# Neighbourhood-attention layer: a cap on the bytes that the attention stage's DMAs have under way

## The chip, the cores and the metric

The kernel runs on one core of a Trainium2 chip. The metric is device time in microseconds (us) of one execution; three timed runs of the kernel before gave 990.62, 991.14 and 992.26 us, median 991.14. A further execution was profiled, and all profile lines come from it.

## The reference

The reference is one pre-norm residual layer (DEPTH is 1, so only mixer A is used) on x of 2048 tokens by 1024 channels in float32, with 16 heads of 64 channels and the tokens laid out as a grid of 32 rows by 64 columns:

```
h = rmsnorm(x, norm_0)
q, k, v, gate = split(h @ w_in_0, 4)             # w_in_0: 1024 x 4096
o = neighbourhood_attention(q, k, v, rpb_0)      # each token: 8 x 16 neighbours of the grid, learned bias
x = x + (o * silu(gate)) @ w_out_0               # w_out_0: 1024 x 1024
return rmsnorm(x, norm_f)
```

Inside the attention each query sees 8 rows by 16 columns of keys; scores get a per-head relative-position bias, a softmax, and weight the values.

## The kernel before

All matmuls work on float32 data that is split into a high and a low float32r part, three products for one. The projections and the output projection use a seven-product (Strassen) scheme on quarters. The order of the instructions is fixed while the program is built: `build` runs through the work once, and a queue of delayed actions (`store(key, lag, f)`, run by `due` as the count of issued matmuls goes on) decides where stores and loads stand between the other instructions.

The program has three stages in time. Up to about 561 us, `stage_one` and `stage_two` make the projections; q, k, the gate and v are stored to DRAM tensors (`qd`, `kd`, `sgd`, `vd`). From 561 to 871 us runs the attention, in `cycles` = 32 cycles of about 9.7 us; from 871 us on, the last part of the output projection (`rows_by_seven`) with the final norm.

In the attention, a cycle m works on one pair of heads p and one quarter T of the tokens, taken from the list `order`. PE does four things in it: some matmuls of the rest of the projections (`group`, tile `pp`, L384 to L388) or, later, of the output projection (tile `po`, L1600 to L1604), as filling; transposes of the normalised probabilities of the cycle before (`turns`, tile `ph`, L1372); the scores of this cycle (`scores`, tile `s`, L1323); and the weighted values of the cycle before (`values`, tile `o`, L1395). These four stand in this order, so the transposes, scores and values form one uninterrupted burst of short matmuls at the end of every cycle. ACT, DVE and POOL do the exponentials, the normalisation and the copies out of PSUM.

The data of a cycle come by DMA from SP's queue. `begin(m)` puts them in the queue at the start of cycle m: the gate tile of the cycle before (`load_sg`, tile `sgt`, L1263), two bias tables (`load_bias`, `em`, L1277), the queries (`load_q`, tile `q`, L1248) and keys (`load_k`, `kt`, L1239) of the next cycle, and the values of this one (`load_v`, `vt`, L1258). Beside them stand the store of the finished tile (`keep`, `ogd<-og`, L1402), loads of weights (`load_item`, `raw`, L161 and L163), and stores of the last projections (`give`, L366 and L373). q, k and v have two buffers each, so a load of q waits until the scores that read its buffer are done, and a load of v until the weighted values that read its buffer are done. Most are of 256 KB; `vt` is 480 KB, `kt` 128 to 512 KB, `em` 184 or 253 KB. From cycle 24 on, finished rows of the attention are loaded back (`load_og`, tile `ograw`, L1429), split by ACT and DVE (`split_og`, L1441) and multiplied by the output weights. In the last cycle nine tiles of prepared weights (`land_first`, tile `t`, L1624) and six tiles of attention rows (`load_rows_of`, `raw<-ogd`, L1656) are loaded for the part after the attention, whose products stand in L1695 and read what `form_rows` (L1661 on ACT, L1662 on DVE) makes of those rows.

SP issues its DMAs strictly in the order of the program. Each DMA signals one of eight semaphores, DMAHW0 to DMAHW7, in turn, and before it is issued it waits for the last DMA on the same semaphore, the one eight places earlier. So at most eight are under way.

Of the kernel before, what the change touches and what calls it, by code (L numbers as in the profile page):

```python
# [31 lines left out]
RES_BUFS, RES_EARLY = 3, 1  # L32
PLAIN = 4

FRAME, TALL = [0, 4, 12, 17], 15
# [26 lines left out]
def build(ctx, tc, x, xr, xt, wg, bias, w_out, n0, nf, out):  # L62
    nc = tc.nc
# [90 lines left out]
    def load_item(it):  # L154
        kind, a, b = it
        t = raws[it] = raw([128, 512], F32, "raw")
        asked_at[it] = now()
        if kind == "x":
            nc.sync.dma_start(t, xt[a * 128:(a + 1) * 128, b * 512:(b + 1) * 512])
        elif kind == "w":  # L160
            nc.sync.dma_start(t, wg[a[0], :, 512 * b:512 * b + 512])  # L161
        else:
            nc.sync.dma_start(t, w_out[a * 128:(a + 1) * 128, b * 512:(b + 1) * 512])  # L163

# [191 lines left out]
    def give(kind, hp, c, t, bank_=False):  # L356
        while sum(e[1][0] in "kqg" for e in later) > 1:
            later.pop(0)[2]()
        s = slice(c * 512, c * 512 + 512)
        written.add((kind, hp, c))  # L360
        to, at = (lambda o: lay(kind, o), of(kind, t)) if bank_ else (lambda o: o, t)
        if kind == "g":
            sg = ev([128, 512], F32, "sg")
            nc.scalar.activation(to(sg), at, AF.Tanh, scale=0.5)
            nc.vector.scalar_tensor_tensor(to(sg), to(sg), 1.0, at, op0=OP.add, op1=OP.mult)
            store(("g", hp, c), 12, lambda: nc.sync.dma_start(sgd[hp][c], sg))  # L366
# [6 lines left out]
        store((kind, hp, c), 12, lambda: nc.sync.dma_start(qd[hp][c] if kind == "q" else kd[hp][:, s], t))  # L373

# [22 lines left out]
    def put_rows(dst, v):  # L397
        nc.sync.dma_start(dst, v.rearrange("p (h d) -> p h d", h=4))

# [13 lines left out]
    def seven_products(us, c0, X1, also):  # L413
# [5 lines left out]
        def load_w(n, f, home=raw):  # L419
            A[n, f] = home([128, 512], F32, "raw")  # L420
            k, j = us[n]
            b = 512 * quarter[f]
            nc.sync.dma_start(A[n, f], wg[KINDS[k] + j, :, b:b + 512])

# [110 lines left out]
    def load_x(c0, f, k, to, cols=slice(0, 512)):  # L535
        r, c = int(f[1]) - 1, int(f[2]) - 1 + c0
        nc.sync.dma_start(to[:, cols], xt[(4 * r + k) * 128:(4 * r + k + 1) * 128, c * 512 + cols.start:c * 512 + cols.stop])

# [48 lines left out]
    def load_s(q, *js):  # L587
        for j in js:
            if q in vsp:
                a, b = j % 2, j // 2  # L590
                if a == 0:
                    W[q, b] = wp([128, 2, 512], F32R, "wh"), wp([128, 2, 512], F32R, "wl")
                for i, t in enumerate(W[q, b]):
                    nc.sync.dma_start(t[:, :, a * 256:a * 256 + 256].bitcast(F32), vsp[q][j, i].rearrange("p (k c) -> p k c", c=256))
                continue
            VR[q, j] = t = raw([128, 512], F32, "raw")
            nc.sync.dma_start(t, wg[KINDS["v"] + 2 + j % 2, :, 1024 + 512 * (j // 2):1536 + 512 * (j // 2)] if q == "A22" else vsd[q][j])

# [18 lines left out]
    def stage_one():  # L617
# [24 lines left out]
        def load_rows(c, hs, p):  # L642
            for h in hs:
                t, j = 4 * c + h // 2, h % 2
                rows_in[t, j] = p([128, 512], F32, "row")
                nc.sync.dma_start(rows_in[t, j], xr[t * 128:t * 128 + 128, 512 * j:512 * j + 512])

# [7 lines left out]
        def value_rows(j):  # L655
            spot = mkp([128, 3, 512], F32, "vs")
            homes = [spot[:, k] for k in range(3)] + [kh([128, 512], F32, "vs")]
            a, b = j % 2, j // 2
            for f, u, h in (("A21", 1, 0), ("A22", 1, 2), ("A11", 0, 0), ("A12", 0, 2)):
                VS[f] = homes.pop()  # L660
                o = 512 * (b + h)
                nc.sync.dma_start(VS[f], wg[KINDS["v"] + 2 * u + a, :, o:o + 512])

        def value_sum(j, f):
            a, b, to, o = {"S1": ("A21", "A22", "A22", OP.add), "S3": ("A11", "A21", "A21", OP.subtract),
                           "S2": ("S1", "A11", "A11", OP.subtract), "S4": ("A12", "S2", "A12", OP.subtract)}[f]
            nc.vector.tensor_tensor(VS[to], VS[a], VS[b], o)
            VS[f] = s = VS[to]
            if f in vsd:
                store(("vs", f, j), 3, lambda: nc.sync.dma_start(vsd[f][j], s))  # L670

        def value_split(j, f):
            h, l = ev([128, 512], F32R, "vsh"), ev([128, 512], F32R, "vsl")
            split_to(h, l, VS[f], None)
            for i, s in enumerate((h, l)):
                store(("vs", f, j, i), 5, lambda i=i, s=s: nc.sync.dma_start(vsp[f][j, i], s.bitcast(F32)))

        def ask_rows(m):
            more_rows[m] = xp([128, 512], F32, "row"), xp([128, 512], F32, "row")
            for j in range(2):  # L680
                nc.sync.dma_start(more_rows[m][j], xr[(8 + m) * 128:(9 + m) * 128, 512 * j:512 * j + 512])

# [113 lines left out]
        for t in range(4):  # L796
            u = ev([128, 512], F32, "u1v")
            nc.scalar.activation(u, ps[t], AF.Copy)
            nc.sync.dma_start(vu1[t], u)
        load_rows(0, range(8), mp)  # L800
# [119 lines left out]
        def load_u1():  # L920
            for t in range(4):
                U1[t] = accs[t] if t < 2 else ep([128, 528], F32, "u1")[:, :512] if t == 2 else kh([128, 512], F32, "u1")
                nc.sync.dma_start(U1[t], vu1[t])

# [86 lines left out]
    def stage_two():  # L1011
# [11 lines left out]
        def out_rows(k):  # L1023
            def g():
# [7 lines left out]
                for q, (r_, c_) in quarters.items():  # L1032
                    OW[q] = homes.pop()
                    nc.sync.dma_start(OW[q], w_out[(4 * r_ + k) * 128:(4 * r_ + k + 1) * 128, c_ * 512:c_ * 512 + 512])
            return g
# [8 lines left out]
        def out_split(k, f):  # L1044
            def g():
# [3 lines left out]
                for i, s in enumerate((h, l)):  # L1049
                    store(("ow", f, k, i), 5, lambda i=i, s=s: nc.sync.dma_start(wod[f][k, i], s.bitcast(F32)))  # L1050
            return g
# [174 lines left out]
    def load_k(p, T):  # L1226
# [5 lines left out]
        def keys():  # L1232
# [4 lines left out]
            if T == 2:  # L1237
                nc.gpsimd.memset(t[:, 1280:1288], 0.0)
            nc.sync.dma_start(t[:, a - base * GW:b - base * GW], kd[p][:, a:b])  # L1239

        return keys

    def load_q(p, T):
        must(("q", p, T))

        def queries():
            QT[p, T] = qp([128, 512], F32, "q")
            nc.sync.dma_start(QT[p, T], qd[p][T])  # L1248

        return queries  # L1250

    def load_v(p, T):
# [4 lines left out]
        VT[p, T] = t.rearrange("p (s d) -> p s d", s=8)  # L1257
        nc.sync.dma_start(t[:8 * TALL], rows)  # L1258

    def load_sg(p, T):  # L1260
        must(("g", p, T))
        SG[p, T] = sp([128, 512], F32, "sgt")
        nc.sync.dma_start(SG[p, T], sgd[p][T])  # L1263

# [3 lines left out]
    def load_bias(p, T):  # L1268
# [4 lines left out]
        for quad in range(2):  # L1273
            t = mp([128, 512], F32, "em")[:, :w]
            EM[p, T // 2, kind].append([t[:, :w // 2], t[:, w // 2:]])
            o = TABLE_AT[kind] + quad * w
            fs.append(lambda t=t, o=o, w=w: nc.sync.dma_start(t, bias[p, 128 * o:128 * (o + w)].rearrange("(q c) -> q c", c=w)))  # L1277
        return fs
# [103 lines left out]
    def values(m):  # L1382
# [18 lines left out]
        def keep():  # L1401
            nc.sync.dma_start(ogd[T][:, p // 4, :, p % 4].rearrange("i a q -> a i q"), og.rearrange("p (i q) -> p i q", i=4))  # L1402
            written.add(("og", p, T))
# [7 lines left out]
    def late_loads():  # L1411
        for j in range(2):
            nc.sync.dma_start(accs[j], bass.AP(tensor=nf.tensor, offset=nf.offset + 512 * j,
                                               ap=[[0, 128], [1, 512]]))
# [10 lines left out]
    def load_og(n):  # L1425
        T, i = divmod(n, 4)
        must(*[("og", p, T) for p in range(NP)])
        G[n] = t = wp([128, NK, 128], F32, "ograw")
        nc.sync.dma_start(t.rearrange("p (h k) q -> p h k q", h=2), ogd[T][i].rearrange("h a k q -> a h k q"))  # L1429

    def load_res(n, j):
        RES[n, j] = rbp([128, 512], F32, "xr")
        nc.sync.dma_start(RES[n, j], x[n * 128:n * 128 + 128, 512 * j:512 * j + 512])

# [186 lines left out]
    def land(where, homes):  # L1621
        for (f, k, i), h in zip(where, homes):
            TF.setdefault(f, [[None, None] for _ in range(4)])[k][i] = h
            nc.sync.dma_start(h.bitcast(F32), wod[f][k, i])  # L1624

# [25 lines left out]
    def load_rows_of(m, f, home=None):  # L1651
# [3 lines left out]
        A[m, f] = (home or raw)([128, 512], F32, "raw")  # L1655
        nc.sync.dma_start(A[m, f].rearrange("p (k q) -> p k q", k=4), ogd[T][i, half])  # L1656

# [12 lines left out]
    def load_rest_of(m):  # L1670
        n = PAIRS[m][0]
        RES[n, 0] = rbp([128, 512], F32, "xr")
        nc.sync.dma_start(RES[n, 0], x[n * 128:n * 128 + 128, :512])

# [150 lines left out]
    for m in range(cycles + 1):  # L1825
        a = amount[m] - 8
        begin(m)
        feed(HALF_HEAD)
# [89 lines left out]
```

## Time and profile before

| | |
|---|---|
| three timed runs | 990.62, 991.14, 992.26 us; median 991.14 |
| the profiled execution | 993.25 us |
| its span, first to last instruction | 991.5 us |
| PE busy | 979.3 us, 99% of the span |
| DVE, ACT, POOL busy | 755.2, 531.5, 159.6 us |
| bytes moved by DMA | 227.93 MB, mean 230 GB/s |
| granted TensorE clock | 0.999 |

Of a row of a DMA listing, the last number is the median time in us from issue to landing. In a list of instructions the first number is the start in us from the start of the span, the second the time in us, and what stands in brackets is how long the engine sat idle before and what ended that. In the chain of work that ended last, "issue" is time in which an engine waited for nothing that the profile shows. A table by stretches gives for each stretch the busy time of each engine with its instructions, the granted clock, the busy share of the DMA engines and the GB/s they moved.

### The profile page before, as it was taken

To read this page: it belongs to the slowest core of one execution; us is meant where nothing else is said; L and a number is where in the kernel's file an instruction comes from. 1 tells how busy PE (TensorE), PEld (TensorE's weight loads), DVE (VectorE), ACT (ScalarE), POOL (GpSimd) and SP (SyncE) were. 2 spreads that over 40 slices of the span, in tenths; PEclk is the share of its full clock that TensorE was granted. 3 is DMA by queue.
4 is the path that set the end of the run, shared out by engine and by line. 5 is a ranking of instruction groups with operands and counts; after the bars stand their busy time and mean duration, and the time that the engine had idled before them with its cause. 6 is when DMAs were issued, how large, how long until landed. Compare 5 with 4: busy or idle time off the path is not lost.

```text
span 991.5 us, 22624 instructions
## 1 busy us (share of the span) xinstructions
PE 979.3 (99%) x8172; PEld 797.0 (80%) x8172; DVE 755.2 (76%) x1735; ACT 531.5 (54%) x1310; POOL 159.6 (16%) x430
## 2 busy tenths in 40 slices
PE   9999999999999999999999999999999999999997
PEld 7888888888888888888888778777778777888886
DVE  6899888988665876766775677668778878877866
ACT  7773245455535342343433467677777776654443
POOL 0000001231100000000001133333343332302110
PEclk9999999999999999999999999999999999999999
DMA  8943547777957836657565799878989978697754
GB/s 287 337 130 102 196 132 256 248 242 251 368 159 225 276 116 201 189 182 224 169 176 203 247 302 271 264 226 279 307 277 288 298 222 266 223 379 212 205 146 117
DMA packets 149968, 227.93 MB, mean 230 GB/s; under 512 B 13536, under 2 KB 66016, under 8 KB 149856
## 3 DMA queue, kind: packets, MB, share of 16 engines
q1 hardware_dynamic: 146832, 221.37, 70.2%
q0 software_dynamic: 2592, 4.72, 2.8%
q8 instruction: 64, 1.05, 0.4%
q14 instruction: 48, 0.39, 0.1%
q10 hardware_dynamic: 432, 0.40, 0.1%
HBM read 160.37 MB, written 66.06 MB: 228 GB/s over the span
## 4 chain that ended last, share of the span: by engine, by line
PE 99%; issue 1%; DVE 0%; ACT 0%
PE pp L446 40%; PE pv L612 13%; PE py L1695 12%; PE o L1395 8%; PE s L1323 6%; PE ph L1372 5%; PE pp L388 2%; PE pp L384 2%; PE pp L386 2%; PE pv L727 2%; PE po L1600 2%; PE po L1604 2%; PE po L1602 2%; PE zp L127 0%; PE prb L235 0%
## 5 line engine op out<-in xcount | busy, mean ns | idle before, releaser
L446 PE MATMUL pp<-h,f 128*128 128x512 f32 x576 | 185.3, 389 | 0.0
L446 PE MATMUL pp<-t,f 128*128 128x512 f32 x702 | 171.4, 389 | 0.0
L446 PEld LDWEIGHTS pp<-t,f 128*128 128x128 f32 x702 | 131.8, 188 | 27.4
L1340 ACT ACTIVATE x<-sums,st 128x264 f32<-128x264 f32 (+1 forms) x256 | 124.5, 488 | 30.0 <-DVE st L1332 30.0
L446 PEld LDWEIGHTS pp<-h,f 128*128 128x128 f32 x576 | 108.1, 188 | 22.6
L446 PE MATMUL pp<-l,f 128*128 128x512 f32 x288 | 112.0, 389 | 0.0
L1352 POOL TENSOR_SCALAR x<-x,st 128x264 f32<-128x264 f32 (+1 forms) x192 | 88.5, 477 | 113.7 <-DVE st L1347 93.8
L1332 DVE CUSTOM_DVE_ANT_0 sums<-s,em 128x253 f32<-128x253 f32 (+1 forms) x256 | 91.1, 401 | 6.2 <-ACT x L1340 1.7
L429 DVE TENSOR_TENSOR f<-raw,f 128x512 fp32r<-128x512 f32 x105 | 75.9, 727 | 19.4 <-ACT f L428 19.3
L1395 PE MATMUL o<-pta,vt 120*64 120x192 f32 (+2 forms) x1152 | 85.1, 300 | 4.0 <-issue 4.0
L1395 PEld LDWEIGHTS o<-pta,vt 120*64 120x64 f32 x1152 | 70.2, 137 | 23.2 <-issue 16.4
L428 ACT ACTIVATE f<-raw 128x512 fp32r<-128x512 f32 x105 | 63.4, 622 | 36.6 <-DVE raw L435 22.0
L1376 DVE COPY pta<-ph 120x512 f32<-120x512 f32 x96 | 60.3, 684 | 18.3 <-PE ph L1372 18.1
L1378 ACT ACTIVATE pta<-ph 120x512 f32<-120x512 f32 x96 | 50.4, 599 | 37.8 <-PE ph L1372 37.8
L446 PEld LDWEIGHTS pp<-l,f 128*128 128x128 f32 x288 | 54.0, 188 | 11.3
L1323 PE MATMUL s<-kt,q 64*32 64x253 f32 (+1 forms) x2048 | 59.2, 362 | 0.7 <-issue 0.7
L1372 PEld LDWEIGHTS ph<-ident,x 64*120 64x120 f32 x1536 | 47.6, 135 | 11.3 <-issue 10.6
L612 PE MATMUL pv<-wh,t 128*128 128x512 f32 x176 | 56.2, 389 | 0.0
L1695 PE MATMUL py<-woh,f 128*128 128x512 f32 x168 | 55.4, 390 | 0.0
L467 POOL TENSOR_TENSOR tmp<-tmp,rb 128x512 f32<-128x512 f32 x18 | 28.5, 1582 | 157.6 <-DVE tmp L464 137.2
L446 PE MATMUL pp<-sixths,f 128*128 128x512 f32 x198 | 52.7, 389 | 0.0
L1372 PE MATMUL ph<-ident,x 64*120 64x64 f32 x1536 | 52.0, 221 | 0.0
(231 smaller groups left out, 1889.4 us busy)
## 6 DMA issues: line engine op xcount, KB each, us to landing
raw<-in_wg_dram SPq DMA_DIRECT2D x124, 256.0 KB, 4.8
vt<-vd SPq DMA_DIRECT2D x32, 480.0 KB, 5.2
row<-in_xr_dram SPq DMA_DIRECT2D x32, 256.0 KB, 5.2
vd<-v SPq DMA_DIRECT2D x32, 256.0 KB, 3.2
sgd<-sg SPq DMA_DIRECT2D x32, 256.0 KB, 3.8
q<-qd SPq DMA_DIRECT2D x32, 256.0 KB, 3.6
sgt<-sgd SPq DMA_DIRECT2D x32, 256.0 KB, 5.3
ogd<-og SPq DMA_DIRECT2D x32, 256.0 KB, 5.3
```

The costliest lines, as they stand in the source:

```text
L428: nc.scalar.activation(t[:, 0], src, AF.Copy)
L429: nc.vector.tensor_tensor(t[:, 1], src, t[:, 0].bitcast(F32), OP.subtract)
L446: nc.tensor.matmul(B[n, P], t[:, int(m == 2), c], x[k][int(m == 1)], start=P in (1, 6, 5) and k == 0 and m == 0, stop=k == 3 and m == 2, s ...
L612: nc.tensor.matmul(p, a[:, o], b, start=P in (1, 6, 5) and k == 0 and m == 0, stop=k == 3 and m == 2, skip_group_check=True)
L1323: nc.tensor.matmul(places[half, s][h * 32:h * 32 + 32], qt[a, g * 64 + half * 32:g * 64 + half * 32 + 32], kt[a, o:o + n * GW].rearrange(" ...
L1332: nc.vector.tensor_tensor_reduce(rows[s][:, :, :WIDE], places[half, s].rearrange("p (r c) -> p r c", c=WIDE), table[s].rearrange("p (r c) ...
L1340: nc.scalar.activation(to, rows[s].rearrange("p r (b c) -> p b r c", b=3), AF.Exp, bias=st[:, o:o + 1], scale=-1.0, accum_out=st[:, 4 + o: ...
L1352: nc.gpsimd.tensor_scalar(t, t, f, 1.0, op0=OP.mult, op1=OP.mult)
L1372: nc.tensor.transpose(ph[h][:k, o:o + 64], X[quad, half, s][q, at:at + k], ident[q, q])
L1376: nc.vector.tensor_copy(o, i_)
L1395: nc.tensor.matmul(o[s * 64:s * 64 + 64, g0 * 64:g1 * 64], vt[:k, strip, s * 64:s * 64 + 64], moving, start=strip == 0, stop=strip == 7, s ...
L1695: nc.tensor.matmul(B[m, P], t[:, a, c], b, start=P in (1, 6, 5) and k == 0 and i == 0, stop=k == 3 and i == 2, skip_group_check=True)
```

## The change

Nearly all DMAs that SP issued directly are now issued through a new helper, `move`. In cycles 1 to 31 of the attention (`paced` is set for 0 < m < cycles) it adds a wait: it goes back over the earlier transfers that went through `move`, newest first, and sums their sizes; the first one with which the sum exceeds 768 KB has to have landed before the new transfer is issued. The new transfer's own size is added to the list only afterwards, so it is not part of that sum. Transfers that don't go through `move` (the final results' stores, L1520, and those of POOL and ACT) aren't counted. Outside the paced cycles `move` issues a DMA as before.

```
+AT_ONCE = 768 * 1024
...
+    paced, under_way = [False], []
+
+    def move(to, from_):
+        d = nc.sync.dma_start(to, from_).ins
+        if paced[0]:
+            left = AT_ONCE
+            for size, earlier in reversed(under_way):
+                left -= size
+                if left < 0:
+                    tc.add_manual_dep(d, earlier.name, mybir.DependencyInfo(mybir.DependencyClass.Sync, mybir.DependencyReason.DATA),
+                                      reason="few bytes under way")
+                    break
+        under_way.append((4 * int(np.prod(to.shape)), d))
+        del under_way[:-8]
...
     def load_sg(p, T):
         must(("g", p, T))
         SG[p, T] = sp([128, 512], F32, "sgt")
-        nc.sync.dma_start(SG[p, T], sgd[p][T])
+        move(SG[p, T], sgd[p][T])
...
     for m in range(cycles + 1):
         a = amount[m] - 8
+        paced[0] = 0 < m < cycles
         begin(m)
```

The other lines of the diff put `move(` in place of `nc.sync.dma_start(` in the same way. The instructions of every engine and their order stay as they were; what changes is what 253 of SP's DMAs, the first issued at 565.97 us and the last at 868.91 us before, wait for.

In the middle of the attention (the store of q at 648.63 us and the seven DMAs after it) SP's rows with the semaphores that each waits for were, before:

```order
L373 DMA qd_66<-q 128x512 [waits DMAHW2_49,Activation_49]
L1263 DMA sgt<-sgd_79 128x512 [waits DMAHW3_49]
L1277 DMA em<-in_bias_dram 128x368 [waits DMAHW4_49]
L1277 DMA em<-in_bias_dram 128x368 [waits DMAHW5_49]
L1248 DMA q<-qd_64 128x512 [waits DMAHW6_49,PE_49]
L1239 DMA kt<-kd_72 128x256 [waits DMAHW7_49]
L1258 DMA vt<-vd_84 120x1024 [waits DMAHW0_49,PE_49]
L1402 DMA ogd_86<-og 128x4x128 [waits DMAHW1_49,DVE_49]
```

The same eight rows on SP now (L80 is the line in `move`):

```order
L80 DMA qd_66<-q 128x512 [waits Activation_49]
L80 DMA sgt<-sgd_79 128x512 [waits DMAHW0_49]
L80 DMA em<-in_bias_dram 128x368 [waits DMAHW4_49]
L80 DMA em<-in_bias_dram 128x368 [waits DMAHW1_49]
L80 DMA q<-qd_64 128x512 [waits DMAHW6_49,DMAHW2_49,PE_49]
L80 DMA kt<-kd_72 128x256 [waits DMAHW3_49]
L80 DMA vt<-vd_84 120x1024 [waits PE_49]
L80 DMA ogd_86<-og 128x4x128 [waits DMAHW6_49,DVE_49]
```

Each DMA's own semaphore is the one that its row before waits for. So `sgt` (semaphore 3) now waits for semaphore 0, the load of `vt` three places ahead; the second `em` (5) and `q` (6) and `kt` (7) wait for the one four places ahead, and a row that names no earlier DMA needs none beyond those already waited for.

At the end of the attention, where the last of the nine weight tiles, the store of `og` and the rows for the part after are loaded, SP had:

```order
L1624 DMA t<-wodT_96 128x512 [waits DMAHW6_49]
L1402 DMA ogd_87<-og 128x4x128 [waits DMAHW7_49]
L1520 DMA out_dram<-y 128x512 [waits DMAHW0_49]
L1520 DMA out_dram<-y 128x512 [waits DMAHW1_49]
L1656 DMA raw<-ogd_87 128x512 [waits DMAHW2_49]
L1656 DMA raw<-ogd_87 128x512 [waits DMAHW7_49,DMAHW3_49]
L1656 DMA raw<-ogd_86 128x512 [waits DMAHW4_49]
```

Now SP has there:

```order
L80 DMA t<-wodT_96 128x512 [waits DMAHW2_49]
L80 DMA ogd_87<-og 128x4x128 [waits DMAHW3_49]
L1536 DMA out_dram<-y 128x512 x2
L80 DMA raw<-ogd_87 128x512 [waits DMAHW4_49]
L80 DMA raw<-ogd_87 128x512 [waits DMAHW7_49,DMAHW5_49]
L80 DMA raw<-ogd_86 128x512 [waits DMAHW6_49]
```

The last weight tile and the store of `og` wait for the DMA four places ahead instead of eight; the first `raw<-ogd` waits for the one six places ahead, since the two stores of results between them are not counted. The second `raw<-ogd` waits, now as before, for that store of `og` (semaphore 7).

More of the change, by code (lines that the diff above doesn't have):

```diff
@@ L365, in give @@
             nc.vector.scalar_tensor_tensor(to(sg), to(sg), 1.0, at, op0=OP.add, op1=OP.mult)
-            store(("g", hp, c), 12, lambda: nc.sync.dma_start(sgd[hp][c], sg))
+            store(("g", hp, c), 12, lambda: move(sgd[hp][c], sg))
             return
@@ L372, in give @@
             nc.scalar.activation(t, t, AF.Copy, scale=HD ** -0.5)
-        store((kind, hp, c), 12, lambda: nc.sync.dma_start(qd[hp][c] if kind == "q" else kd[hp][:, s], t))
+        store((kind, hp, c), 12, lambda: move(qd[hp][c] if kind == "q" else kd[hp][:, s], t))
     def group(w, a, c, n):
@@ L669, in value_sum @@
             if f in vsd:
-                store(("vs", f, j), 3, lambda: nc.sync.dma_start(vsd[f][j], s))
+                store(("vs", f, j), 3, lambda: move(vsd[f][j], s))
         def value_split(j, f):
@@ L1049, in g @@
                 for i, s in enumerate((h, l)):
-                    store(("ow", f, k, i), 5, lambda i=i, s=s: nc.sync.dma_start(wod[f][k, i], s.bitcast(F32)))
+                    store(("ow", f, k, i), 5, lambda i=i, s=s: move(wod[f][k, i], s.bitcast(F32)))
             return g
@@ L1257, in load_v @@
         VT[p, T] = t.rearrange("p (s d) -> p s d", s=8)
-        nc.sync.dma_start(t[:8 * TALL], rows)
+        move(t[:8 * TALL], rows)
     def load_sg(p, T):
@@ L1655, in load_rows_of @@
         A[m, f] = (home or raw)([128, 512], F32, "raw")
-        nc.sync.dma_start(A[m, f].rearrange("p (k q) -> p k q", k=4), ogd[T][i, half])
+        move(A[m, f].rearrange("p (k q) -> p k q", k=4), ogd[T][i, half])
     def form_rows(m, P):
```

48 lines of the change are left out of this document (24 added, 24 removed).

## The prediction

> **What bounds the kernel now.** I read the page's busy times, then the chain of waits for the attention (561 to 871 us), then the DMA listings around what stood out there.
>
> ```profile
> PE 979.3 (99%) x8172; PEld 797.0 (80%) x8172; DVE 755.2 (76%) x1735; ACT 531.5 (54%) x1310; POOL 159.6 (16%) x430
> PE 99%; issue 1%; DVE 0%; ACT 0%
> ```
>
> PE sets the time, and no load is on its chain. So a DMA change can gain only where PE stands still, and lose wherever it makes PE wait. PE is idle for 991.5 - 979.3 = 12.2 us. In the attention the chain shows these pieces:
>
> ```profile
> 588.55 2.06 issue
> ...
> 626.25 0.35 issue
> ...
> 662.67 0.74 issue
> ...
> 728.41 0.88 issue
> ...
> 794.34 0.74 issue
> ```
>
> 2.06 + 0.35 + 0.74 + 0.88 + 0.74 = 4.77 us in which PE waits for no semaphore, always inside the burst of short matmuls (`s`, `o`). The rest of the idle time lies at the program's two ends, which the change doesn't touch. What PE lacks shows in the DMA listing: a queue that carries instructions. The rows are of the whole program, the attention, and the windows 588 to 588.5, 624 to 625 and 726.5 to 727.5 us:
>
> ```profile
> q8 instruction: 64, 1.05, 0.4%
> q8 instruction: 41, 0.67, 0.8%
> q8 instruction: 1, 0.02, 12.2%
> q8 instruction: 1, 0.02, 6.1%
> q8 instruction: 1, 0.02, 6.5%
> ```
>
> One packet of 16 KB (1.05 MB / 64) comes every 310 / 41 = 7.6 us in the attention, and one begins just before each of these three gaps. I read the gaps as PE having run out of instructions because a refill came late. A refill shares the DMA engines with the data, and they are crowded just there:
>
> ```profile
> DMA packets 53085, 83.60 MB, mean 270 GB/s; under 512 B 4546, under 2 KB 29897, under 8 KB 53020
> q1 hardware_dynamic: 53020, 82.74, 85.9%
> ...
> vt<-vd SPq DMA_DIRECT2D x32, 480.0 KB, 5.2
> ...
> q<-qd SPq DMA_DIRECT2D x31, 256.0 KB, 3.5
> ...
> kt<-kd SPq DMA_DIRECT2D x8, 512.0 KB, 4.8
> ```
>
> The engines are 86% busy with SP's data. `q`, issued when little is under way, lands in 3.5 us; `vt`, with more under way, needs 5.2. Why loads come in bursts shows one cycle, SP first, then PE:
>
> ```profile
> 644.97 0.33 SPq L1248 DMA_DIRECT2D q<-qd  x1
> 645.34 0.43 SPq L1239 DMA_DIRECT2D kt<-kd  x1
> 647.44 0.34 SPq L1258 DMA_DIRECT2D vt<-vd  x1
> ...
> 649.13 0.46 SPq L1263 DMA_DIRECT2D sgt<-sgd  x1
> 649.64 1.53 SPq L1277 DMA_DIRECT2D em<-in_bias_dram  x2
> 653.44 0.33 SPq L1248 DMA_DIRECT2D q<-qd  x1
> ```
> ```profile
> 644.85 2.55 PE o L1395 x36
> ...
> 660.81 1.86 PE s L1323 x62
> ...
> 664.02 2.00 PE o L1395 x27
> ```
>
> `q` goes out the moment the scores end (644.85), everything behind it within 6.2 us, and then SP is idle (651.17 to 653.44) until the next scores are done.
>
> **The change part by part.** The diff adds one wait to 253 DMAs. Its sum leaves out the new transfer itself, so with 256 KB each it lets four be under way, 1 MB, not three; with the semaphore ring it was eight, 2 MB. Instructions and order stay the same on every engine.
>
> *Refills (gain, 0 to 4.77 us).* With at most four or five transfers queued on each engine, a refill finds about half of the data ahead of it in the worst case. The gaps are the tail of a distribution: 41 refills, five late, four of those by under 0.9 us and one by 2.06. Half the queue saves more than that: four transfers of 256 KB at the mean 270 GB/s are 1.05 MB / 270 = 3.9 us. The ends are no gain (a refill waits for something else) and all 4.77. I take 4.0, nearer to the whole, because the missing time is small beside 3.9 us, but a steadier queue leaves fewer quiet moments to slip into.
>
> *What waits behind the new wait.* SP runs in order, so a held DMA holds all behind it. In the cycle above `sgt` must now wait for `vt`, which in this cycle (window 641 to 650 us) took
>
> ```profile
> vt<-vd SPq DMA_DIRECT2D x1, 480.0 KB, 5.7
> ```
>
> so it goes out at 647.44 + 5.7 = 653.1 instead of 649.13, 4.0 us later, and the two `em` (0.5 us of issue each) and the next `q` behind it about 2 us after 653.44. Who waits for that? The `q` issued at 644.97 fills the buffer that the scores had just read; the scores of 651.7 use the other one, and it is read at 660.81: 15.8 us after issue, 12.3 after landing. `vt`, issued at 647.44, is read at 664.02: 16.6 - 5.7 = 10.9 us to spare. One cycle's 2 to 4 us is hidden. What counts is whether the lateness grows from cycle to cycle.
>
> *Does it grow?* Bytes asked for against what 1 MB under way can carry. In five stretches of the attention:
>
> ```profile
> 670.00:695.00 25.00, 25.00 (x475) 20.13 (x472) 20.60 (x78) 19.73 (x64) 9.89 (x37) 1.00 0.91 283
> 695.00:720.00 25.00, 25.00 (x465) 19.85 (x465) 20.12 (x71) 18.84 (x56) 8.02 (x31) 1.00 0.96 303
> 720.00:745.00 25.00, 24.12 (x386) 19.06 (x384) 17.75 (x67) 17.68 (x58) 9.95 (x32) 1.00 0.89 276
> 745.00:770.00 25.00, 25.00 (x457) 20.12 (x452) 21.80 (x80) 20.57 (x66) 10.02 (x38) 1.00 0.89 279
> 770.00:795.00 25.00, 24.34 (x450) 19.02 (x450) 21.72 (x74) 19.21 (x57) 7.76 (x31) 1.00 0.92 290
> ```
>
> The last number is GB/s moved. No row shows a steady four under way, so I bound the capacity: four 256 KB in `q`'s 3.5 us is 1.05 MB / 3.5 = 300 GB/s; four in the 4.8 us of `kt`, as if its queueing stayed, is 218; the best of these stretches had 303. At 300 the lateness grows only in the second stretch, by 3 x 25 = 75 KB, 0.3 us: hidden. At 265 it grows in all five, by (18 + 38 + 11 + 14 + 25) x 25 = 2650 KB, 10.0 us, about the 10.9 us that `vt` has to spare. I take 280 to 300, since `q`'s latency is the one seen with a short queue: nothing on PE's chain from lateness alone.
>
> SP has the room for it: in the attention it waited for PE
>
> ```profile
> SPq L1248 <- PE s L1323: 66.9, 25, 5.4
> SPq L1258 <- PE o L1395: 46.9, 29, 7.2
> ```
>
> 113.8 of 310 us; a held DMA, and the instruction that holds it, eat that first.
>
> *Two tight places.* The first rows loaded back from the attention:
>
> ```profile
> 727.52 0.37 SPq L1429 DMA_DIRECT2D ograw<-ogd  x1
> 733.11 1.14 ACT L1441 ACTIVATE gh<-ograw 128x512 fp32r<-128x512 f32 x2
> ograw<-ogd SPq DMA_DIRECT2D x1, 512.0 KB, 3.4
> ```
>
> It lands at 730.9, 2.2 us before ACT reads it. At 300 GB/s the lateness is under 1 us there; beyond 2.2 us ACT stands, and has 25 - 17.68 = 7.3 us idle in that stretch to make it up. I count 0 (at 265 up to 3 us). The second is the end of the attention:
>
> ```profile
> 868.46 0.63 ACT L1661 ACTIVATE f<-raw 128x512 fp32r<-128x512 f32 x1 [0.73 <-DMA raw<-ogd]
> 869.13 0.69 DVE L1662 TENSOR_TENSOR f<-raw,f 128x512 fp32r<-128x512 f32 x1 [0.21 <-ACT f L1661]
> 870.74 114.58 PE py L1695 x504
> ```
>
> ACT already waits for `raw<-ogd`; DVE is done at 869.82 and PE's first product starts at 870.74, 0.9 us to spare. The nine weight loads ahead of it are now issued four at a time. If the engines stay full, it lands as before (0; earlier would gain nothing, since PE doesn't wait there). If the hand-overs empty the engines for the time of a transfer, once before the store of `og` and once before its load, that is 2 x 256 KB / 270 GB/s = 1.9 us, 1.0 of it on the path. I take 0.9 for this place and what else is small.
>
> *Sum.* The profiled execution took 993.25 us (span 991.5): 993.25 - 4.0 + 0.9 = 990.15. It lies 2.1 us above the median of the timed runs, 991.14, so for those -3.1 us: **988.0**.
>
> [...]
>
> **The rivals.**
>
> *Slower: the cap is too small.* If the capacity with four under way is below about 262 GB/s, where the lateness over 670 to 795 us passes the 10.9 us to spare, SP falls behind for good and PE waits for `vt` and `kt`. At 250 the five stretches leave (33 + 53 + 26 + 29 + 40) x 25 = 4525 KB, 18.1 us, of which 10.9 are hidden: +7.2, and with the refills' 4.0 regained 991.14 + 3.2 + 0.9 = 995; with late refills as well 999. At 240 it is 5775 KB, 24.1 us, +13.2: about 1001. At the bound of 218, 83.6 MB need 383 us in place of 310: +62, which I hold unlikely, since `kt`'s 4.8 is for 512 KB. For it: the mean demand, 270, is close to the threshold. Against: short-queue latency of 3.5 us.
>
> *No change: refills don't care.* The gaps stay because a refill's wait isn't set by how much data is queued, or the refills improve and the tight places take it back: 991.14 + 0.9 - (0 to 2) = 990 to 992. For it: DMA stays as busy on average, since the same bytes move in the same time. Against: the gaps all lie where transfers pile up.
> [...]
>
> *It doesn't do what it says.* The limit is 1 MB and more, not 768 KB; if even that seldom binds, nothing moves, 991. Little for it: in the cycle above everything from `sgt` to the last `em` is issued before `vt` lands at 653.1.
>
> **How the numbers follow.** A difference of under 0.2% (2 us) can hardly be told from none here. Gaps gone for the most part and no new wait: 0.48, time 986.3 to 989.1 (all of 4.77 gone is 986.4). Within 2 us, from the second and third rivals and a gain that small stalls eat: 0.24. Slower, 993.2 to 1001 for capacities of 260 to 240, with a thin tail beyond: 0.28. The likeliest is 988.0; its own range is 986.3 to 990. The range for 8 in 10 takes in no change and the slower case at 250 GB/s: 986.3 to 996.
>
> **What would show it.** Right: the pieces called issue in the attention's chain shrink from 4.77 us to about 1; SP's waits in the attention are for DMAs and those for PE scores (66.9 us) shrink; `vt` and `sgt` land in 3 to 4.5 us; the stretch 670 to 795 us takes no longer. Wrong: PE or PEld waiting for `vt`, `kt` or `ograw` after 727 us, the first matmul of L1695 later relative to the last `o`, or the five gaps of unchanged size.

## The result and the profile after

The kernel with the cap took 1033.81 us (median of four runs, 1031.61 to 1038.04) against 991.7 for the kernel before (990.62 to 993.01): ratio 1.0429, 95% interval 1.0391 to 1.0467. It is slower by 42 us, and far outside the forecast of 986.3 to 996.0. The profiled execution took 1032.72 us, with a span of 1030.9.

The page of after, busy times and the chain that ended last:

```profile
PE 985.9 (96%) x8172; PEld 803.1 (78%) x8172; DVE 751.9 (73%) x1735; ACT 532.2 (52%) x1310; POOL 160.5 (16%) x430
PE 80%; DMA 15%; DVE 2%; issue 1%; ACT 1%; SPq 0%; POOL 0%; DVEq 0%; ACTq 0%
```

Before, DMA had no share of the chain; now it is 15%. The attention as one stretch, of before (first fence) and of after (second), shows where the time came from. The columns are the stretch, busy time of PE, PEld, DVE, ACT and POOL, the granted clock, the DMA engines' share and GB/s.

```profile
561.00:871.00 310.00, 305.24 (x5212) 241.52 (x5211) 241.80 (x883) 225.30 (x707) 110.38 (x378) 1.00 0.87 270
```
```profile
561.00:908.00 347.00, 309.40 (x5214) 246.46 (x5212) 240.04 (x883) 225.19 (x706) 110.42 (x378) 0.98 0.80 239
```

And from the chain of after, the last stage's products (start, length):

```profile
907.96 116.82 PE py L1711 x504
```

The attention ends at 907.96 in place of 870.74, 37.2 us later, and the part behind it takes 116.82 in place of 114.58, 2.2 us more; together they are the 39.4 us by which the span grew. Inside the attention PE stands idle for 347 - 309.40 = 37.6 us (before 4.8), and is busy for 4.2 us longer with the same work. The same bytes move at 239 GB/s in place of 270, while the DMA engines are busy for less of the time (0.80). So the engines are not what is full; the queue is not given enough.

What PE and SP wait for in the attention of after, both from the list of waits (total us, times, longest):

```profile
PE s L1339 <- DMA kt<-kd: 9.6, 8, 2.0
PE s L1339 <- ACT pta L1394: 6.9, 1, 6.9
PE py L1711 <- ACT f L1677: 6.6, 1, 6.6
PE o L1411 <- DMA vt<-vd: 5.6, 5, 1.6
PE o L1411 <- ACT x L1356: 2.8, 4, 1.3
PE ph L1388 <- POOL x L1368: 2.7, 4, 1.2
PE s L1339 <- issue: 1.4, 1, 1.4
...
SPq L80 <- DMA vt<-vd: 55.4, 31, 4.7
SPq L80 <- DMA kt<-kd: 45.6, 23, 4.6
```

Before, PE waited only for "issue":

```profile
PE o L1395 <- issue: 4.0, 4, 2.1
PE s L1323 <- issue: 0.7, 1, 0.7
```

and SP waited mostly for PE (66.9 and 46.9 us). Now the order is turned round: SP's waits in the new line L80 are nearly all for transfers, and PE waits for `kt` and `vt` that came late. The two single waits of 6.9 and 6.6 us belong to the two tight places that the prediction named. The chain of the first, in order of time:

```profile
736.69 4.82 DMA vt<-vd
...
741.57 0.32 SPq L80
...
741.94 4.04 DMA sgt<-sgd
...
746.00 4.93 DMA kt<-kd
...
750.99 2.38 DMA ogd<-og
...
753.39 3.48 DMA ograw<-ogd
...
756.89 1.15 ACT gh L1457 x2
758.04 0.49 ACT pta L1394
```

Each transfer starts when an earlier one has landed, so a row of SP's queue becomes a chain: 20 us in which five transfers follow one another. The last step is not the cap's: `ograw` reads what `ogd<-og` has stored, and waited for it before as well, for 4.8 us. ACT reaches the split of `ograw` (`gh`) and stands for 9.5 us; behind it, in ACT's order, is the copy of `pta`, and PE waits for that.

During this pause the granted clock falls (it stands third from the end of each row):

```profile
745.00:750.00 5.00, 4.35 (x60) 3.35 (x58) 1.18 (x4) 1.02 (x5) 1.75 (x7) 1.00 0.95 277
750.00:755.00 5.00, 0.58 (x2) 0.14 (x2) 0.00 (x0) 0.00 (x0) 0.00 (x0) 0.73 0.48 145
755.00:760.00 5.00, 1.42 (x32) 0.86 (x40) 2.44 (x5) 2.61 (x5) 0.00 (x0) 0.50 0.88 301
760.00:765.00 5.00, 5.00 (x83) 3.28 (x68) 3.73 (x21) 3.79 (x15) 1.61 (x4) 0.75 0.66 200
765.00:770.00 5.00, 5.00 (x77) 4.03 (x85) 3.31 (x8) 2.69 (x7) 1.63 (x8) 1.00 0.64 219
```

1.00 before the pause of 6.9 us, 0.50 at its end (758.58), full again at 762.5. The same happens at the end of the attention (0.59 from 905 to 910 us). The 2.2 us that the part behind the attention takes longer lie there: its first nine products took 4.21 us, where nine take 2.1 us later on. Of the 4.2 us inside the attention the clock explains less than half: the 62 score matmuls right after the pause took 3.62 us, where 64 of them took 1.94 at 605 us. What the rest is stays open.

Three theories stood at this point. Theory 1: with so few bytes under way the queue moves less than the attention needs, SP falls behind for good, and everything else follows. Theory 2: something that comes with the cap costs, the added waits themselves or the other engines' traffic, which slows the transfers. Theory 3: the mean rate doesn't matter; the loss is the two places without slack and the clock after them.

### The profile page after: what moved, and what is told of

It is laid out like the page before. It is cut to its first block, busy times and chain, and to the rows that moved or that the text cites. A ratio compares the mean times of both kernels' runs of the same rounds, so it can differ in the third digit from the quotient of the medians.

```text
span 1030.9 us, 22624 instructions
## 1 busy us (share of the span) xinstructions
PE 985.9 (96%) x8172; PEld 803.1 (78%) x8172; DVE 751.9 (73%) x1735; ACT 532.2 (52%) x1310; POOL 160.5 (16%) x430
## 4 chain that ended last, share of the span: by engine, by line
PE 80%; DMA 15%; DVE 2%; issue 1%; ACT 1%; SPq 0%; POOL 0%; DVEq 0%; ACTq 0%
PE pp L462 39%; PE pv L628 13%; PE py L1711 11%; DMA vt<-vd 4%; PE o L1411 4%; DMA sgt<-sgd 4%; PE s L1339 3%; PE pv L743 2%; DMA kt<-kd 2%; PE ph L1388 2%; DMA ogd<-og 1%; PE pp L400 1%; PE pp L404 1%; PE pp L402 1%; DMA em<-in_bias_dram 1%
## 5 line engine op out<-in xcount | busy, mean ns | idle before, releaser
L444 ACT ACTIVATE f<-raw 128x512 fp32r<-128x512 f32 x105 | 63.5, 622 | 37.2 <-DVE raw L451 21.7
L1339 PEld LDWEIGHTS s<-kt,q 64*32 64x32 f32 x2048 | 39.1, 108 | 28.9 <-issue 10.6
```

What stands on the lines that cost most here:

```text
L444: nc.scalar.activation(t[:, 0], src, AF.Copy)
L1339: nc.tensor.matmul(places[half, s][h * 32:h * 32 + 32], qt[a, g * 64 + half * 32:g * 64 + half * 32 + 32], kt[a, o:o + n * GW].rearrange(" ...
```

## Experiments

### The cap's size

The edit, with 1024, 1536, 2048 and 3072 KB (and later 512 and 1280):

```
-AT_ONCE = 768 * 1024
+AT_ONCE = 1024 * 1024
...
-        del under_way[:-8]
+        del under_way[:-16]
```

> The cap is raised from 768 to 1024 KB (each issue may add its own size on top: five transfers of 256 KB under way in place of four). Theory 1, too few bytes under way lower what the queue moves, and the attention is bound by it: in the trace of before the queue moved 262 to 267 GB/s while 800 to 1300 KB were under way, against a need of 270, so at 255 to 262 GB/s the attention's 83 MB take 317 to 326 us in place of 310: 999 to 1008 us. Theory 2, the 291 added waits cost by themselves: the count is the same, so about 1030 us. Theory 3, the loss is in a few places with no slack (the load of ograw, the rows at the end, the clock after them) while the rest is hidden: the two long waits of 6.9 and 6.6 us shrink by a fifth with the delay, about 1025 us.

> The cap is 1536 KB: seven transfers of 256 KB under way. Theory 1: the trace of before shows 277 to 294 GB/s at 1300 to 2000 KB under way, over the need of 270: 990 to 997 us. Theory 2, the added waits themselves cost: about 1030 us. Theory 3, only places with no slack: the delays that the cap makes are a sixth of those at 768 KB if replayed on the times of before (71 of 457 us), so about 997 us. Whether the pauses of TensorE that nothing explains (4.8 us in the attention before) shrink with fewer bytes under way: by the forecast's reason some would be gone, and the time could fall to 988 us.

> The cap is 2048 KB. Replayed on the times of before it holds back 7 issues by 7 us in all. Theory 1 and theory 3: 990 to 993 us. Theory 2, the added waits themselves: about 1030 us. The pauses of TensorE that nothing explains: as before, 4 to 5 us.

> The cap is 3072 KB, more than was ever under way before (2784 KB): the waits stand in the program and never hold anything back. Theories 1 and 3: 991 us, as before. Theory 2, the added waits themselves: about 1030 us.

> The cap is 1280 KB. Theory 1: the mix alone moved 267 GB/s with this cap, the attention's mean need is 265 to 267, so it is at the limit: the stretches that need 285 to 300 fall behind and are caught up later; 992 to 997 us. The pauses of TensorE that nothing explains: 2 to 4 us, as the bytes under way are only a little fewer.

> The cap is 512 KB. Theory 1: the mix alone moved 212 GB/s with this cap, so the attention's 82 MB take 388 us in place of 310; with 5 to 10 us more for the falls of the granted clock after long waits and for the end: 1074 to 1082 us. Theory 3 (places with no slack): the waits there grow by the longer delay, some 5 us more than at 768 KB, about 1040 us.

The rates in the third column are those of the next experiment; "pauses" is the sum of PE's waits called issue in the attention of the one profiled execution.

| cap, KB | us | the loads alone, GB/s | ratio to before, 95% interval | pauses, us |
|---|---|---|---|---|
| 512 | 1083.47 | 211 | 1.0927 [1.0884, 1.0970] | hidden in other waits |
| 768 (the change) | 1033.81 | 238 | 1.0429 [1.0391, 1.0467] | 1.4 |
| 1024 | 1008.04 | 255 | 1.0165 [1.0131, 1.0199] | 0.9 |
| 1280 | 995.07 | 267 | 1.0033 [1.0012, 1.0055] | 4.0 |
| 1536 | 994.23 | 299 | 1.0023 [1.0010, 1.0036] | 7.0 |
| 2048 | 993.06 | 289 | 1.0009 [0.9993, 1.0026] | 3.1 |
| 3072 | 992.32 | 307 | 1.0003 [0.9989, 1.0017] | 3.5 |
| none (before) | 992.05 | 307 | | 4.7 |

The run at 3072 KB is a control and, against its expectation, says nothing of the waits: with so large a cap the transfer to be waited for lies so far back that SP has waited for it anyway, and in the trace only 2 of SP's 284 DMAs in the attention wait for another DMA's semaphore than their own, as many as before, where the kernel with 768 KB has 211 of 277. At 1536 KB it is 203 of 276, and the kernel takes some 2 us more than before, which the rate, 299, doesn't explain. So the waits by themselves cost 2 us at most, and that half of theory 2 is out. The loss beyond these 2 us starts where the loads alone fall below the 270 GB/s that the attention needs, and theory 1's times hold to within 1.5 us at every size (at 512 KB, 1074 to 1082 expected, 1083 measured). Theory 3 missed 1024 KB by 17 us and 512 KB by 43. It has a share, though: at 1024 KB the two tight places are most of what is left. PE's waits there:

```profile
PE s L1339 <- ACT pta L1394: 5.8, 1, 5.8
PE py L1711 <- ACT f L1677: 3.9, 1, 3.9
PE s L1339 <- DMA kt<-kd: 3.5, 3, 1.5
PE s L1339 <- issue: 0.5, 1, 0.5
PE o L1411 <- issue: 0.4, 1, 0.4
```

9.7 of these 14.1 us lie in two waits, both at the end of a store to `ogd` and a load back from it.

### The loads by themselves

A kernel of its own: SP's queue and nothing else. Per stretch:

```
    for name, n in (("one", 1), ("two", 2), ("three", 3), ("four", 4), ("five", 5), ("six", 6), ("eight", 8), ("twelve", 12)):
        first[0], cap[:] = True, [n, None]
        for k in range(32 if n < 2 else 56):
            move(rows([128, 512], F32, name), block(wg, k))
    for name, c in (("B", 512), ("C", 768), ("D", 1024), ("E", 1280), ("F", 1536), ("G", 2048), ("H", None)):
        first[0], cap[:] = True, [None, c and c * 1024]
        for m in range(8):
...
```

> Leaves out all computation: no engine but the queue of SP works, and the output is not the reference's. Eight stretches load 128x512 tiles (256 KB) with at most 1, 2, 3, 4, 5, 6, 8 and 12 under way; seven more issue the attention's own mix of one cycle after another (sgt, two tables em, q, kt, vt, a tile of w_out, the store to ogd), with caps of 512, 768, 1024, 1280, 1536 and 2048 KB and none, counted as the change counts them. Theory 1 (bytes under way set what the queue moves, whoever else works): the mix gives about 236 GB/s at 768 KB, 255 at 1024, 263 to 270 at 1280 and 1536, and over 280 at 2048 and with none, as the attention did. Theory 2 (the other engines' work slows the transfers, and the cap would be harmless by itself): at 768 KB the mix reaches the 280 to 300 GB/s of the forecast. For plain tiles by the forecast's reason (1 MB in 3.5 us) four under way give 300 GB/s; by theory 1 at most 260.

The stretches of that kernel; the first three rows are plain tiles with one, four and eight under way, the others the attention's mix at 512, 768, 1024, 1280 KB and with no cap:

```profile
103.50:185.60 82.10, 0.00 (x0) 0.00 (x0) 1.00 0.37 102
...
323.40:375.70 52.30, 0.00 (x0) 0.00 (x0) 1.00 0.87 281
...
466.70:507.50 40.80, 0.00 (x0) 0.00 (x0) 1.00 1.00 360
549.00:636.10 87.10, 0.00 (x0) 0.00 (x0) 1.00 0.73 211
636.40:713.70 77.30, 0.00 (x0) 0.00 (x0) 1.00 0.81 238
714.10:786.30 72.20, 0.00 (x0) 0.00 (x0) 1.00 0.92 255
786.70:855.70 69.00, 0.00 (x0) 0.00 (x0) 1.00 0.94 267
...
982.10:1042.10 60.00, 0.00 (x0) 0.00 (x0) 1.00 1.00 307
```

238 GB/s at 768 KB, with every other engine still: the attention's 239 is the queue's own rate under this cap, and theory 2 is out altogether. Four plain tiles under way move 281, landing after 3.6 us each: for these the forecast's 280 to 300 was right. The mix is what it doesn't hold for. One plain tile at a time moves 102 GB/s and lands after 2.6 us; with eight under way one lands every 0.73 us (256 KB at 360 GB/s). So most of the 2.6 us is time in which other transfers can move, only overlap brings the rate, and the cap is a cap on overlap.

### Which kind of transfer pulls the mix down

The same kernel with other stretches, the mix as it is, four with one thing in it changed, and ten with one or two kinds alone:

```
+    cases = dict(
+        A=lambda c: whole(c),
+        B=lambda c: whole(c, vt=0),
+        C=lambda c: whole(c, n=128),
...
+        E=lambda c: whole(c, vt=2, kt=1 if c.T == 0 else 2),
+        F=lambda c: [c.sgt() for _ in range(8)],
...
+    for name, f in cases.items():
+        first[0], cap[:] = True, [None, 768 * 1024]
+        for m in range(8):
+            f(parts(m, name))
```

> Leaves out all computation, so that the output is not the reference's. Fifteen stretches, all with the cap of 768 KB counted as the change counts it: the attention's mix; the mix without vt; with vt as 128 rows of partitions in place of 120; without the store to ogd; with kt and vt cut into two transfers each; then each kind alone: sgt, the tables of 253 KB, those of 184 KB, kt of 484 KB, kt of 128 KB, vt of 120 partitions, vt of 128 partitions, a tile of w_out, the store to ogd, sgt and ogd in turn. Theory 1 in its general form (what is under way and how long a transfer takes set the rate): the mix 238 GB/s again, sgt alone 290 as plain tiles with four under way. Which kind pulls the mix down: if the size of the steps (a transfer of 480 KB leaves room for two more in place of four), the mix with cut kt and vt reaches 270 and each kind of 256 KB alone stays near 290; if vt's 120 partitions, vt alone lies under 230 and with 128 partitions over 260; if the short pieces of ogd and of the tables, these alone lie under 230 and the mix without ogd over 250.

Again the loads alone, all at 768 KB. Rows: the mix; without `vt`; with `vt` as 128 rows of partitions; with `kt` and `vt` cut in two; then alone `sgt`, `kt` of 484 KB, `vt` of 120 partitions, `vt` of 128, the store to `ogd`:

```profile
104.30:180.70 76.40, 0.00 (x0) 0.00 (x0) 1.00 0.83 241
181.00:235.90 54.90, 0.00 (x0) 0.00 (x0) 1.00 0.86 264
236.20:309.50 73.30, 0.00 (x0) 0.00 (x0) 1.00 0.84 255
...
377.20:447.20 70.00, 0.00 (x0) 0.00 (x0) 1.00 0.87 263
447.60:506.00 58.40, 0.00 (x0) 0.00 (x0) 1.00 0.88 287
...
610.20:695.00 84.80, 0.00 (x0) 0.00 (x0) 1.00 0.77 234
747.00:841.80 94.80, 0.00 (x0) 0.00 (x0) 1.00 0.76 207
842.20:926.10 83.90, 0.00 (x0) 0.00 (x0) 1.00 0.78 250
...
989.60:1049.30 59.70, 0.00 (x0) 0.00 (x0) 1.00 0.99 281
```

The short pieces of `ogd` are no cause (281 alone, and the mix without it moves 243), nor are the tables (281 and 274 alone). `vt` is the slowest kind (207), `kt` the next (234); with both cut in two, or with `vt` gone, the mix reaches 263 or 264. Under this cap two of these large transfers are under way at a time, or four of 256 KB. Both the size of the steps and `vt`'s 120 partitions count: 128 partitions lift `vt` alone from 207 to 250 and the mix to 255. The expectation's 270 for the cut mix was a little high. `kt` of 128 KB alone says nothing on the cap, since its four buffers held it back; it is left aside.

### Fewer bytes to move

Half of the cycles reuse the q, vt and sgt of the cycle before, without the cap (light_free, where AT_ONCE is too large ever to bind) and with it (light_768):

```
-        t = vp([128, 1024], F32, "vt")
-        VT[p, T] = t.rearrange("p (s d) -> p s d", s=8)
-        move(t[:8 * TALL], rows)
+        if T in (1, 2):
+            last["vt"] = vp([128, 1024], F32, "vt")
+            move(last["vt"][:8 * TALL], rows)
+        VT[p, T] = last["vt"].rearrange("p (s d) -> p s d", s=8)
```

> No cap. In half of the cycles the loads of q, vt and sgt are left out and the tiles of the cycle before are used again, so that the output is not the reference's: 16 MB of the attention's 82 MB are gone, and 66 MB in 310 us need 213 GB/s. All theories: no more than before, 986 to 991 us (the 4.8 us of TensorE's unexplained pauses may shrink with fewer bytes moved).

> The same with the cap of 768 KB. Theory 1: the need of 213 GB/s is under the 236 that the queue moves with this cap, so most of the loss is gone: 0 to 8 us over the kernel without the cap. Theory 3 (the loss is in the two places with no slack and in the clock after them, which each wait for one load's own way, not for the sum): 13.5 us of waits and about 4 of the clock stay, 17 us over it.

light_free took 989.05 us (ratio to before 0.9965 [0.9949, 0.9982]), light_768 took 987.88 (0.9959 [0.9947, 0.9970]). The same cap that costs 42 us costs nothing once the attention needs less than the queue moves, though 180 of the 247 DMAs in its attention carry an added wait. It even takes 1.2 us off (ten runs each, 986.89 to 988.67 us with it and 987.63 to 990.05 without), about the 1.1 us of pauses called issue that light_free has and light_768 has not. Both tight places lost their waits as well, so theory 3 falls as a theory of its own: a load there is late because SP is behind, not because its own way got longer. The attention of light_768:

```profile
561.00:870.00 309.00, 309.00 (x5236) 245.97 (x5236) 248.59 (x899) 228.61 (x714) 110.41 (x378) 1.00 0.75 228
```

PE is busy for 309.00 of 309 us, and 228 GB/s move, under the 238 that the cap allows. The pauses called issue are gone (4.7 us in before).

### One half of the attention

The cap in cycles 1 to 15 only; in the other kernel the condition is `16 <= m < cycles`:

```
-        paced[0] = 0 < m < cycles
+        paced[0] = 0 < m < 16
```

> The cap of 768 KB holds in the first 15 cycles of the attention only. Theory 1: TensorE's gaps up to there (14.6 us in the trace of after, against 4.0 before) come, about 1002 us, less what the uncapped half wins back from loads that were late. Theory 3, the loss is in the two places of the second half: 992 us.

> The cap of 768 KB holds from the attention's cycle 16 on. Theory 1: what the first half did not cost, 42 less 24 us, so about 1010 us; the long wait near ograw falls away or is short, since SP comes to it without a lag. Theory 3: all of the places with no slack are in this half, so nearly the whole loss but the first half's 10 us: 1020 us or more.

The first half alone took 1016.76 us (1.0263 [1.0235, 1.0291]), the second alone 1014.23 (1.0224 [1.0185, 1.0264]). Both theories' numbers for the first half were too low (1002 and 992). The expectation had counted PE's idle time up to the end of that half only, but SP's queue is still late when the cap ends, and a pause of 4.7 us near `ograw` and the clock after it follow. There the store that `ograw` waits for landed after 7.15 us, among loads that catch up at 354 GB/s (740 to 745 us); before, the same store took 5.3. For the second half theory 1 said about 1010 and theory 3 1020 or more; 1014.23 lies between them, and the long wait near `ograw` fell away, as theory 1 had it. That the two losses add up to 46 us, near the 42 of the whole, is what a rate that is too low does, and not what two places in the second half would do.

### vt and kt in two transfers each, in the kernel

```
-        move(t[:8 * TALL], rows)
+        for k in (slice(0, 512), slice(512, 1024)):
+            move(t[:8 * TALL, k], rows[:, k])
...
+            cuts = 2 if b - a > 512 else 1
+            for k in range(cuts):
+                f, l = a + (b - a) * k // cuts, a + (b - a) * (k + 1) // cuts
+                move(t[:, f - base * GW:l - base * GW], kd[p][:, f:l])
```

> The change as it is, but each vt and each kt of over 128 KB goes as two transfers (two halves of the columns). Theory 1 with the large transfers as what pulls the mix down: the mix alone moved 263 GB/s in place of 241 when these two kinds were cut, so the attention's 82 MB take 312 us, close to what it needs (310): 993 to 999 us, most of the 42 us won back. If vt and kt matter only in the loads alone and not in the kernel: 1028 to 1034 us, as uncut.

> The same with a cap of 1024 KB (uncut, 1008 us). Theory 1: scaled as at 768 KB (255 by 263/241) 278 GB/s, over the need: TensorE no longer waits for loads. If the pauses that nothing explains shrink with the bytes under way, as they did with fewer loads (none in the capped, 1.1 us in the uncapped light kernel), 3 to 4 us of the 4.8 go: 987 to 990 us, faster than before. If they do not: 991 to 993 us.

> The same with a cap of 1280 KB. Theory 1: 267 by 263/241 is 291 GB/s, no waits for loads. The pauses that nothing explains shrink less than at 1024 KB: 988 to 992 us.

> vt and kt cut in two, and no cap: the control for the three others. 991 to 993 us, as before; the pauses that nothing explains 4 to 5 us as before.

| cap, KB | uncut, us | cut, us | cut: ratio to before, 95% interval |
|---|---|---|---|
| 768 | 1033.81 | 1015.68 | 1.0239 [1.0215, 1.0264] |
| 1024 | 1008.04 | 994.47 | 1.0013 [1.0002, 1.0025] |
| 1280 | 995.07 | 989.63 | 0.9964 [0.9948, 0.9980] |
| none | 992.05 | 989.35 | 0.9972 [0.9960, 0.9984] |

At the same cap the size of the single transfer alone takes back 18 of 42 us, so that the large transfers do cost the kernel time, and not only the loads alone; but the expectation of 993 to 999 was missed. The attention of cut_768 moved less than the 263 GB/s of the loads alone (first fence), and its longest waits were again the two tight places (second fence):

```profile
561.00:870.00 309.00, 292.59 (x4958) 231.17 (x4957) 229.54 (x846) 216.47 (x680) 108.09 (x372) 0.98 0.80 250
```
```profile
PE s L1343 <- ACT pta L1398: 6.7, 2, 6.3
PE s L1343 <- DMA kt<-kd: 6.3, 4, 2.9
PE py L1715 <- ACT f L1681: 5.3, 1, 5.3
```

Why 250 and not 263 wasn't tried. At 1024 KB one wait of 4.0 us for `ograw`, still one transfer of 512 KB, was nearly all that was left. At 1280 KB PE is never idle for a wait in the attention, and without a cap for 1.3 us; these two are faster than the kernel before, by some 3 us, and equal to each other. Cutting is the gain, and the cap adds nothing that was measured: the version to take from this study has `vt` and `kt` in two transfers each and no cap, 989.35 us.

Where the bytes under way were bounded at 768 KB, `vt` and `kt` in halves moved more than whole: 263 GB/s in place of 241 in the mix, 250 in place of 239 in the attention. With no bound the kernel was no slower with the halves (989.35 us against 992.05).

## Why the prediction was wrong

**The step that failed** is the capacity: "I take 280 to 300, since `q`'s latency is the one seen with a short queue". It is 238. The trace had a bound below it in view, 218 from `kt`'s 4.8 us, and I set it aside because `kt` is a large transfer. But 32 `vt` of 480 KB and 15 large `kt` are 32 x 0.49 + 8 x 0.52 + 7 x 0.50 = 23 of the attention's 82 MB, and a large transfer under a cap in bytes isn't neutral: `vt` alone moves 207 where `q`'s kind moves 287. Nor was `q`'s queue short: in the trace of before, 1136 KB were under way when a `q` was issued in the attention (median of 31). And "lets four be under way, 1 MB" is a peak, not a mean. Worked out over all of SP's transfers that land in the attention of after (bytes by time from the start of the issue to landing, as the DMA listings count it, over the stretch), 985 KB were under way, each byte for 4.27 us and not for `q`'s 3.5; before it was 1371 KB and 5.29 us. The issue of a transfer that was held ended 0.39 us after the landing it waited for (median of some 180), and that time is lost from the overlap at each step.

**The rival that came true was priced too low.** At 240 GB/s it gave 1001; 1034 came. It took the lateness of five stretches (24.1 us) and subtracted 10.9 us to spare. But at 240 the queue is below the mean need of 270, so it is late over the whole attention, and the slack helps once: 83.6 MB / 240 = 348 us in place of 310 is +38, less what the slack hides. The same sum was made rightly one line below, at 218. The measured attention, 347 us, is this quotient, and the 238 GB/s that go into it were measured by the loads alone. The flat row of rates shows it: in the stretches where before moved 276 to 303, after moved 229 to 245. What was missing besides was the fallen clock behind the attention, 2.2 us; the 4.2 us of longer work inside it are part of the 347.

**The pauses shrank, and it was too little to matter.** The pauses called issue, forecast to fall by 4.0 of 4.77 us, fell by 3.4. That alone doesn't show the reason given for it: PE stood for 37.6 us in this attention, much of it for loads, and a refill can arrive meanwhile. At 1024 KB they were 0.9, with fewer bytes 1.1, with fewer bytes and the cap, or cut at 1280 KB, none. With the uncut transfers and 1280 KB or more they stayed at 3 to 7 us, in single executions. They stand at the same places of the program where PE's instructions are the same (588.55, 626.25 and 662.67 us before; 588.92 and 625.19 in the cut kernel without a cap), which fits refills, though no row of a trace names what PE lacked there. So the reading that the refills wait for data ahead of them holds up as far as these sums go, against the rival that they don't care; but most of the fall came with fewer or smaller transfers, not with the cap on the bytes under way, since these without a cap left 1.1 and 1.3 us. Whether a large transfer holds a refill up, and by what, no run shows.

**The hidden lateness.** `vt` was said to have 10.9 us to spare and `q` 12.3. That holds for one cycle; PE waited for `kt` at 8 places and for `vt` at 5. SP's 113.8 us of waiting for PE were indeed used up, and what followed was more.

**The two tight places** were the right ones: 6.9 and 6.6 us. I counted 0 and 0.9, as the lateness arriving there was taken as under 1 us. What the prediction listed as signs of being wrong (PE waiting for `vt`, `kt` or `ograw` after 727 us, a later first product of the last stage) is what the trace shows, except that the waits for loads begin at 603 us.

**Landing times.** "3 to 4.5 us" held for `sgt` (3.7) and not for `vt` (5.1): with 985 KB under way in place of 1371, a transfer of 480 KB took nearly as long as before (5.2).

## What to carry to other kernels

Before a queue is capped, the rate that it keeps under the cap is to be measured with the kernel's own mix of transfers, by the loads alone in one small kernel, and set against the mean need of the stage. Here the cap of 768 KB, which moves 238 GB/s, cost nothing where the attention moved 228 (987.88 us with it, 989.05 without); where it needed 270, the attention took 347 us, about bytes divided by rate, and slack helped only once. The latency of one kind of transfer didn't give that rate (`q`'s 3.5 us gave 300), and the bound in bytes was worth less with larger single transfers (`vt` of 480 KB alone 207 GB/s, `sgt` of 256 KB 287). A queue whose engines were 80% busy was the bound.

## What the runs showed of the hardware

- Plain tiles of 256 KB in one queue: 102 GB/s with one under way, 281 with four, 360 with eight.
- Loads of 120 partitions by 4 KB moved 207 GB/s under the cap of 768 KB (two under way), loads of 128 partitions by 4 KB 250.
- The granted clock was 0.50 in the 5 us in which a pause of PE of 6.9 us ended, and full again 3.9 us after its end. In the kernel with the cap it stood at 0.50 for 10.24 us from 752.3 on and for 6.83 us from 905.9 on, and at 1.00 between the two. It fell after shorter pauses too: in the cut kernel at 1024 KB it was 0.66 from 737 to 742 us, behind a pause of 4.0 us. In the capped first half, PE stood for 2.06 us at 785 us; the row with this pause and the two behind it are:

```profile
784.00:787.00 3.00, 0.99 (x35) 0.47 (x19) 1.70 (x9) 2.06 (x9) 0.00 (x0) 1.00 0.29 96
787.00:790.00 3.00, 2.95 (x39) 2.24 (x41) 1.45 (x10) 1.71 (x7) 1.22 (x3) 0.73 0.41 116
790.00:793.00 3.00, 3.00 (x20) 2.13 (x17) 1.18 (x4) 0.65 (x4) 0.90 (x3) 0.70 0.22 41
```

The kernel before kept its full clock (1.00 in the rows from 588 to 594 us) through a pause of the same 2.06 us at 588.55 us, and the kernel with the cap after one of 1.7 us at 603 us. So the length of the pause alone didn't decide it; what else does wasn't tried.
